# Moving the second input group of each FFN ahead of the first group's turn

## The chip, the cores and the metric

The kernel runs on 1 core of one Trainium2 chip. The metric is device time in microseconds (us) of one execution. Before the change the median of 3 runs is 1911.91 us (1911.91 to 1919.89).

## The reference

The program is a two-layer transformer-like block in fp32 on 256 tokens of width 1024, followed by a second two-layer block. Only the feed-forward networks (FFN) of the first block and what joins them to their neighbours matter here; there are four, two in each layer, with 2816 hidden features:

```python
def rmsnorm(x, g):
    xf = x.astype(jnp.float32)
    y = xf * lax.rsqrt(jnp.mean(xf * xf, axis=-1, keepdims=True) + EPS)
    return (y * g.astype(jnp.float32)).astype(x.dtype)

def swiglu(x, w_in, w_out):
    gate, up = jnp.split(x @ w_in, 2, axis=-1)
    return (jax.nn.silu(gate) * up) @ w_out
...
    for i in range(DEPTH):
        g = norm_g[i]
        h = h + 0.5 * rmsnorm(swiglu(rmsnorm(h, g[0]), ffn1_w_in[i], ffn1_w_out[i]), g[1])
        u = rmsnorm(h, g[2])
        j = i // 2
        if i % 2 == 0:
            mix = even_mixer(u, even_w_in[j], even_w_out[j], lb_all[j], hgrn_onorm_g[j], attn_sinks[j], cos_b, sin_b)
        else:
            mix = odd_mixer(u, odd_w_in[j], odd_w_out[j], ret_onorm_g[j], cos_c, sin_c)
        h = h + rmsnorm(mix, g[3])
        h = h + 0.5 * rmsnorm(swiglu(rmsnorm(h, g[4]), ffn2_w_in[i], ffn2_w_out[i]), g[5])
        gate = jax.nn.sigmoid(h @ ple_w_gate[i])
        h = h + rmsnorm(gate * (p[i] @ ple_w_proj[i]), g[6])
```

The second block (pooling mixer, attention, two squared-ReLU MLPs) follows. Its adaptive scales, a product of a vector with a large matrix (`adw`), are worked out in the background of the first block.

## The kernel before

**Products.** Every fp32 product is made of three matmuls on halves of the operands. `split` loads a 128x1024 piece of weights (raw tile, SP's queue), casts it on ACT to the high half `wh` (line 232) and subtracts on DVE to get the low half `wl` (two instructions, line 235). `mm3` (lines 239 to 241) issues high x high, high x low, low x high. The weight ring holds 7 split pieces, the raw ring 4.

**The normalised input.** A residual update ends in a `junction`: for each of the two rows of 128 tokens (t = 0, 1), `step(t)` squares the result on ACT (`rstd`, line 291, tile jkm), multiplies and adds on DVE (tiles yt and h) and calls `feed`. That transposes h on PE (tile tps) and writes high and low halves of the feature-major input xT (lines 335 and 336), multiplied by the norm's gain but not yet by the row's scale 1/rms. The scale comes from `stats(x, t)`: one square of the whole row with its sum on ACT (line 343, tile jkg), then an addition and a power on POOL (lines 344 and 345, tile rx). In the kernel before, both calls of `stats` stand at the end of step(1), tied behind the last copy of the feed on ACT. The argument `act` adds a one-element activation (`warm`, line 352) behind the feed of t = 0, to load a function table; the junction of the PLE block of layer 0 gives it, that of the even mixer does not.

**An FFN** (`ffn`) has 11 pairs of 128 hidden features. The first pair is worked out token-major: `group512` makes gate and up for 256 features in tile g (a PSUM accumulator), ACT applies silu with the row's scale (line 467), DVE multiplies (line 468, tile sil), and `t_split` transposes the result on PE (line 416) and splits it into hid (lines 244 and 245). The last step is called the turn of the first group in the title; it waits for x.r. Then `rb_of` spreads the scales over a tile rb: two diagonal tiles dg on DVE (line 400), two fp32 products with ones on PE (line 401, tile rbp; four entries in the profile) and a copy on ACT (line 403). The other ten pairs (`inp`) are feature-major: for each of two halves j a bank finm takes 48 matmuls (two weight pieces), DVE multiplies by rb (line 482), ACT applies silu (line 483), DVE multiplies by the up half (line 484), and the result is split into hid. The output of a pair (`out_kn`, tile acc, 24 matmuls) follows one pair behind.

**Buffers.** finm, rbp and all tps come from one pool of two PSUM banks (`pwk`); a bank is free again when its last reader is through. g and acc share another pool of two. sil has 2 buffers.

**Order.** The order of the instructions in each engine's queue is made by a planner from the order of the program (a lower place comes first), the dependences and its own reckoning of durations; a queue, once made, runs in that order. `issue_after` adds an edge within an engine's queue.

**In the background**, `side_ada` streams pieces of `adw` (raw tile rawa, 2 buffers) through DVE (line 974, tile jka) beside each FFN, with a low place in the order, after a silu of the vectors sv on ACT (line 979).

The printed lines are those of the profile.

Of the kernel before, what the change touches and what calls it, by code (L numbers as in the profile page):

```python
# [9 lines left out]
F32 = mybir.dt.float32  # L10
# [3 lines left out]
AF = mybir.ActivationFunctionType  # L14
ALU = mybir.AluOpType
# [154 lines left out]
def tile_model(ctx: ExitStack, tc: tile.TileContext, A, out):  # L170
    nc = tc.nc
    V, S, G, T, Y = nc.vector, nc.scalar, nc.gpsimd, nc.tensor, nc.sync
# [70 lines left out]
    def hilo(hi, lo, src):  # L243
        ins = S.activation(hi, src, AF.Copy)  # L244
        V.tensor_tensor(lo, src, hi.bitcast(F32), op=ALU.subtract)  # L245
        return ins.ins
# [5 lines left out]
    def bank(r=None, name="bk"):  # L252
        r = r or M
        return r.bank.tile([128, 512], F32, name=name + r.tag, tag="bk" + r.tag)
# [25 lines left out]
    def gload(row):  # L280
        return bc(row, 1024, tp, "gb", tag="gb", bufs=1)

    def stat(name):
        return tp.tile([128, 1], F32, name=name, tag=name, bufs=10 if name == "ex" else 6)

    def ssq2(halves, scale):
        sm = small(2, "sm2")
        for n in range(2):
            r = cur[0]
            jk = r.small.tile([128, 512], BF16, name="jk" + r.tag, tag="jk" + r.tag, bufs=1)  # L290
            S.activation(jk, halves[n], AF.Square, scale=scale, accum_out=sm[:, n:n + 1])
        return sm

    def ms_r(sm, e, st=False):
        ms = stat("msx") if st else small(1, "ms")
        V.scalar_tensor_tensor(ms, sm[:, 0:1], sm[:, 1:2], e, op0=ALU.add, op1=ALU.add)
        r = stat("rx") if st else small(1, "rs")
        ins = G.tensor_tensor(r, ms, nhalf[:, :1], op=ALU.pow)
        return ms, r, ins.ins if hasattr(ins, "ins") else ins

    def halves(x):
        return [x[:, 512 * n:512 * n + 512] for n in range(2)]
# [36 lines left out]
    def stats(x, t):  # L339
        if x.stats:  # L340
            sm, ms, r = stat("smx"), stat("msx"), stat("rx")
            jk = tp.tile([128, 1024], BF16, name="jkg", tag="yt", bufs=3)
            S.activation(jk, h[:, t], AF.Square, scale=1.0 / 32, accum_out=sm)
            G.tensor_scalar(ms, sm, EPS, None, op0=ALU.add)
            G.tensor_tensor(r, ms, nhalf[:, :1], op=ALU.pow)
            x.ms[t], x.r[t] = ms, r

    def after(ins):
        return tc.issue_after(ins) if ins is not None else nullcontext()

    def warm(f):
        S.activation(dummy[:, 0:1], dummy[:, 1:2], f)

    def junction(acc, gb, mul, e, x, g, pre=None, act=None):
        def rstd(t):
            sm = ssq2(halves(acc[t]), 1.0 / (32 * mul))
            return ms_r(sm, e[t] if e is not None else epst[:, (0 if mul == 1.0 else 1):(1 if mul == 1.0 else 2)])[1:]

        def scaled(t, n):
            sl = slice(512 * n, 512 * n + 512)  # L360
            y = tp.tile([128, 512], F32, name="yt", tag="yt", bufs=3)
            V.tensor_tensor(y, acc[t][:, sl], gb[:, sl], op=ALU.mult)
            return y

        def add(t, n, y, r):
            sl = slice(512 * n, 512 * n + 512)
            return V.scalar_tensor_tensor(h[:, t, sl], y, r, h[:, t, sl], op0=ALU.mult, op1=ALU.add).ins

        done_ = [None]

        def step(t):
            with after(done_[0]):
                if pre is not None:
                    pre(t)
                r, _ = rstd(t)
                ys = [scaled(t, n) for n in range(2)]
                for n in range(2):
                    with after(done_[0]):
                        done_[0] = add(t, n, ys[n], r)
                    if x.xt is not None:  # L380
                        ins = feed(x, t, n, g)
            if x.xt is not None and t == 0:
                with tc.issue_after(ins):
                    if act is not None:
                        warm(act)
            if t == 1:
                if x.xt is None:
                    for t in range(2):
                        stats(x, t)
                elif x.stats:  # L390
                    with tc.issue_after(ins):
                        for t in range(2):
                            stats(x, t)
        return step

    def rb_of(x):
        ps = bank(name="rbp")
        for t in range(2):
            dg = tp.tile([128, 128], F32, name="dg", tag="dg", bufs=2)
            V.tensor_scalar(dg, ident, x.r[t], None, op0=ALU.mult)  # L400
            T.matmul(ps[:, 128 * t:128 * t + 128], ones, dg, start=True, stop=True)
        rb = tp.tile([128, 256], F32, name="rb", tag="rb", bufs=1)
        S.activation(rb, ps[:, 0:256], AF.Copy)
        return rb
# [6 lines left out]
    def t_split(src, nk, xt, t, k0=0, r=None):  # L411
        for q in range(0, nk, 4):
            n = min(4, nk - q)
            ps = bank(r, "tps")
            for i in range(n):
                T.transpose(ps[:, 128 * i:128 * i + 128], src[:, 128 * (q + i):128 * (q + i) + 128], ident)
            p3 = ps[:, :128 * n].rearrange("p (k c) -> p k c", c=128)
            sl = (slice(None), slice(k0 + q, k0 + q + n), slice(128 * t, 128 * t + 128))
            hilo(xt[0][sl], xt[1][sl], p3)

    def acc_tiles():
        return [pacc.tile([128, 1024], F32, name="acc", tag="acc") for _ in range(2)]
# [35 lines left out]
    def ffn(x, win, wout, np_, pool, hooks, joint):  # L458
        def first():
            hid = xt_tiles(2, pool, "hid", 4)  # L460
            ps = group512(win[0:2], x.xt, True)
            for t in range(2):
                if x.r[t] is None:
                    stats(x, t)
            for t in range(2):
                s = pool.tile([128, 256], F32, name="sil", tag="sil", bufs=2)
                S.activation(s, ps[:, t, 0:256], AF.Silu, scale=x.r[t])
                V.tensor_tensor(s, s, ps[:, t, 256:512], op=ALU.mult)
                t_split(s, 2, hid, t)
            return hid  # L470

        hids = [first()]
        rb = rb_of(x)

        def inp(i):
            hid = xt_tiles(2, pool, "hid", 4)
            for j in range(2):
                ps = bank(name="fin")
                for u in range(2):
                    feat_tile(ps[:, 256 * u:256 * u + 256], split(M, win[2 * i + j], u), x.xt)  # L480
                s = pool.tile([128, 256], F32, name="sil", tag="sil", bufs=2)
                V.tensor_tensor(s, ps[:, 0:256], rb, op=ALU.mult)
                S.activation(s, s, AF.Silu)
                V.tensor_tensor(s, s, ps[:, 256:512], op=ALU.mult)  # L484
                hilo(hid[0][:, j, :], hid[1][:, j, :], s)
            return hid

        acc = None
        for i in range(1, np_):
            hids.append(inp(i))  # L490
            if i in hooks:
                hooks[i](pool)
            if acc is None:
                acc = acc_tiles()
            k = i - LAG
            if 0 <= k < np_ - 2 - XF:
                out_kn(wout[k], acc, hids[k], 0, k == 0, False)
        for k in range(np_ - LAG, np_ - 2 - XF):
            out_kn(wout[k], acc, hids[k], 0, k == 0, False)
        out_multi([(wout[j], hids[j], 0) for j in range(np_ - 2 - XF, np_)], acc, False, True, joint(acc), XF, pool)  # L500
# [112 lines left out]
    def even_block(l, x, nx, ng):  # L613
# [5 lines left out]
        with tc.tile_pool(name="ev", bufs=1, reuse_waits="tile") as ev:  # L619
# [214 lines left out]
            gb = gload(A["norm_g"][l, 3])  # L834
# [3 lines left out]
            for b in range(2):  # L838
# [3 lines left out]
            acc = acc_tiles()  # L842
            x2 = nx()
            out_kn(A["evo"][0], acc, yts[0], 0, True, False)
            out_kn(A["evo"][2], acc, ys, 0, False, False)
            out_multi([(A["evo"][3], ys, 2), (A["evo"][1], yts[1], 0)], acc, False, True,
                      junction(acc, gb, 1.0, None, x2, ng))
        return x2

    def odd_block(l, x, nx, ng):  # L850
# [682 lines left out]
    x = new_x()  # L1533
# [15 lines left out]
    for l in range(2):  # L1549
        x = ffn_block(l, 1, x, new_x, gcol[:, l, 1], cuts[l, 1], None if l else {2: setup, 5: rope2})  # L1550
        x = (odd_block if l else even_block)(l, x, new_x, gcol[:, l, 2])
        x = ffn_block(l, 2, x, plain, None, cuts[l, 2], {5: fin0} if l else None)
# [33 lines left out]
        x = ple_block(l, x, last if l else new_x, None if l else gcol[:, 1, 0], mid if l else None)  # L1586
# [27 lines left out]
```

## Time and profile before

| what | value |
|---|---|
| median of 3 runs | 1911.91 us (1911.91 to 1919.89) |
| the profiled execution | 1917.58 us, span of its instructions 1915.7 us |
| PE (matmul) busy | 1840.0 us, 96% of the span |
| DVE busy | 1336.4 us, 70% |
| ACT busy | 924.9 us, 48% |
| POOL busy | 57.1 us, 3% |
| mean granted TensorE clock | 0.990 |
| read from HBM | 353.03 MB, 185 GB/s over the span |

The page is of one execution; its own time and not the median belongs to its rows. Matmul ends are modelled, so that a busy PE can be a PE that waits within a matmul; stretches of idle time and the granted clock are measured. The four FFNs lie at about 9 to 200, 323 to 517, 552 to 752 and 953 to 1152 us of the span.

### The profile page before, as it was taken

How to read it: one execution, taken by the hardware profiler on the slowest of the kernel's cores; microseconds unless marked ns; L12 is line 12 of the kernel's file. 1: busy time of each engine (PE TensorE's matmuls, PEld its weight loads, DVE VectorE, ACT ScalarE, POOL GpSimd, SP SyncE). 2: the span in 40 equal slices, each digit the busy share in tenths (PEclk: the TensorE clock that was granted, in tenths of full speed). 3: DMA queues.
4: the chain of work that ended last, by engine and by line, in shares of the span. 5: the costliest groups of instructions: out<-in, count | busy, mean ns of one | idle time of the engine just before them, and what ended most of it. 6: DMA issues, size and time to landing. Idle time of an engine off the chain costs nothing.

```text
span 1915.7 us, 29706 instructions
## 1 busy us (share of the span) xinstructions
PE 1840.0 (96%) x11425; PEld 1616.8 (84%) x11425; DVE 1336.4 (70%) x2531; ACT 924.9 (48%) x1452; POOL 57.1 (3%) x96
## 2 busy tenths in 40 slices
PE   8999999999989999999989999899999999999998
PEld 6999777899869998788789897798899987667997
DVE  7997767998679976765587767854444468656555
ACT  6544766544474445444454355632232335544443
POOL 0000000000000000000000000100000002000000
PEclk9999999999999999999999999999999999999999
DMA  8886534887568866655588867332333324216662
GB/s 281 287 280 224 174 112 145 272 285 250 176 205 275 280 215 203 212 168 164 162 275 287 296 207 263 122 121 92 97 91 108 100 67 134 90 56 188 198 191 84
DMA packets 100949, 356.06 MB, mean 186 GB/s; under 512 B 12248, under 2 KB 13128, under 8 KB 100808
## 3 DMA queue, kind: packets, MB, share of 16 engines
q1 hardware_dynamic: 100088, 353.30, 56.8%
q8 instruction: 89, 1.46, 0.3%
q10 hardware_dynamic: 720, 0.88, 0.1%
q14 instruction: 52, 0.43, 0.1%
HBM read 353.03 MB, written 1.10 MB: 185 GB/s over the span
## 4 chain that ended last, share of the span: by engine, by line
PE 77%; DVE 8%; DMA 7%; ACT 3%; issue 2%; POOL 1%; SPq 0%; POOLq 0%; ACTq 0%; DVEq 0%
PE acc L239 8%; PE acc L241 8%; PE acc L240 8%; PE finm L239 6%; PE finm L240 6%; PE finm L241 6%; DMA rawa<-in_adw_dram 4%; PE mfinm L239 3%; PE mfinm L240 3%; PE mfinm L241 3%; DVE wlm L235 3%; PE g L239 2%; PE g L241 2%; PE g L240 2%; PE cfof L239 2%
## 5 line engine op out<-in xcount | busy, mean ns | idle before, releaser
L235 DVE TENSOR_TENSOR wlm<-rawm,whm 128x512 fp32r<-128x512 f32 x1048 | 682.7, 685 | 326.0 <-ACT whm L232 323.2
L232 ACT ACTIVATE whm<-rawm 128x1024 fp32r<-128x1024 f32 x524 | 549.6, 1058 | 522.7 <-PE acc L241 139.7
L239 PE MATMUL finm<-xTh,whm 128*128 128x256 f32 x1280 | 359.9, 281 | 5.4 <-DVE sil L484 5.4
L240 PE MATMUL finm<-xTl,whm 128*128 128x256 f32 x1280 | 359.2, 281 | 0.0
L241 PE MATMUL finm<-xTh,wlm 128*128 128x256 f32 x1280 | 359.1, 281 | 0.0
L239 PEld LDWEIGHTS finm<-xTh,whm 128*128 128x128 f32 x1280 | 240.7, 188 | 8.6 <-DVE sil L484 7.1
L241 PEld LDWEIGHTS finm<-xTh,wlm 128*128 128x128 f32 x1280 | 245.1, 192 | 0.0
L240 PEld LDWEIGHTS finm<-xTl,whm 128*128 128x128 f32 x1280 | 240.4, 188 | 1.3
L239 PE MATMUL acc<-whm,hidh 128*128 128x512 f32 x544 | 214.4, 394 | 2.6 <-ACT hidh L244 2.6
L974 DVE SCALAR_TENSOR_TENSOR jka<-rawa,sv 128x1024 bf16<-128x1024 f32 x160 | 194.9, 1218 | 30.9 <-DMA rawa<-in_adw_dram 29.8
L241 PE MATMUL acc<-whm,hidl 128*128 128x512 f32 x544 | 214.1, 394 | 0.0
L240 PE MATMUL acc<-wlm,hidh 128*128 128x512 f32 x544 | 213.8, 393 | 0.0
L239 PE MATMUL g<-whm,xTh 128*128 128x512 f32 x320 | 130.6, 408 | 10.8 <-ACT xTh L335 4.2
L240 PE MATMUL mfinm<-xTl,whm 128*128 128x256 f32 x480 | 132.6, 276 | 0.0
L241 PE MATMUL mfinm<-xTh,wlm 128*128 128x256 f32 x480 | 132.6, 276 | 0.0
L239 PE MATMUL mfinm<-xTh,whm 128*128 128x256 f32 x480 | 132.6, 277 | 0.0
L241 PE MATMUL g<-whm,xTl 128*128 128x512 f32 x320 | 130.5, 408 | 0.3 <-DVE xTl L250 0.2
L240 PE MATMUL g<-wlm,xTh 128*128 128x512 f32 x320 | 128.7, 402 | 0.0
L239 PEld LDWEIGHTS acc<-whm,hidh 128*128 128x128 f32 x544 | 103.1, 190 | 24.3 <-ACT hidh L244 4.3
L241 PEld LDWEIGHTS acc<-whm,hidl 128*128 128x128 f32 x544 | 102.8, 189 | 21.3 <-DVE hidl L245 0.5
L240 PEld LDWEIGHTS acc<-wlm,hidh 128*128 128x128 f32 x544 | 103.0, 189 | 20.6 <-DVE wlm L235 0.3
L240 PEld LDWEIGHTS mfinm<-xTl,whm 128*128 128x128 f32 x480 | 90.2, 188 | 0.6
(466 smaller groups left out, 3125.9 us busy)
## 6 DMA issues: line engine op xcount, KB each, us to landing
rawm<-in_m_dram SPq DMA_DIRECT2D x128, 512.0 KB, 3.8
rawa<-in_adw_dram SPq DMA_DIRECT2D x96, 512.0 KB, 5.6
rawm<-in_f1i_dram SPq DMA_DIRECT2D x88, 512.0 KB, 4.9
rawm<-in_f2i_dram SPq DMA_DIRECT2D x88, 512.0 KB, 4.9
rawm<-in_odi_dram SPq DMA_DIRECT2D x48, 512.0 KB, 4.2
rawm<-in_f1o_dram SPq DMA_DIRECT2D x40, 512.0 KB, 6.0
rawm<-in_f2o_dram SPq DMA_DIRECT2D x40, 512.0 KB, 5.3
rawm<-in_evi_dram SPq DMA_DIRECT2D x22, 512.0 KB, 4.1
```

What stands on the lines that cost most here:

```text
L232: S.activation(wh, src, AF.Copy)
L235: V.tensor_tensor(wl[:, sl], src[:, sl], wh[:, sl].bitcast(F32), op=ALU.subtract)
L239: T.matmul(o, a[0], b[0], start=first, stop=False)
L240: T.matmul(o, a[0], b[1], start=False, stop=False)
L241: T.matmul(o, a[1], b[0], start=False, stop=last)
L974: V.scalar_tensor_tensor(jk, src, 1.0, sv[v], op0=ALU.mult, op1=ALU.mult, accum_out=adacol[:, l, v, 2 * i + f:2 * i + f + 1])
```

## The change

In `ffn` the turn is cut off from `first()` and called after the input part of the second pair, `inp(1)`; `rb_of` is called within `inp(1)`, behind the matmuls of its first half. The sil tile gets four buffers in place of two. In `junction`, where x is fed, the `stats` of row 0 is called within step(1), behind the squares of that step, and only that of row 1 stays behind the last feed. The junction of the even mixer is given act=Silu. The first FFN makes its scales in `first()`, before and after the change. The rest is as before.

```diff
@@ junction, step(t)
                 r, _ = rstd(t)
+                if t == 1 and x.xt is not None and x.stats:
+                    stats(x, 0)
                 ys = [scaled(t, n) for n in range(2)]
...
                 elif x.stats:
                     with tc.issue_after(ins):
-                        for t in range(2):
-                            stats(x, t)
+                        stats(x, 1)
@@ ffn
+            ss = []
             for t in range(2):
-                s = pool.tile([128, 256], F32, name="sil", tag="sil", bufs=2)
+                s = pool.tile([128, 256], F32, name="sil", tag="sil", bufs=4)
                 S.activation(s, ps[:, t, 0:256], AF.Silu, scale=x.r[t])
                 V.tensor_tensor(s, s, ps[:, t, 256:512], op=ALU.mult)
-                t_split(s, 2, hid, t)
-            return hid
-
-        hids = [first()]
-        rb = rb_of(x)
+                ss.append(s)
+
+            def turn():
+                for t in range(2):
+                    t_split(ss[t], 2, hid, t)
+            return hid, turn
+
+        h0, turn = first()
+        hids = [h0]
+        rbs = []
...
-                s = pool.tile([128, 256], F32, name="sil", tag="sil", bufs=2)
-                V.tensor_tensor(s, ps[:, 0:256], rb, op=ALU.mult)
+                s = pool.tile([128, 256], F32, name="sil", tag="sil", bufs=4)
+                if not rbs:
+                    rbs.append(rb_of(x))
+                V.tensor_tensor(s, ps[:, 0:256], rbs[0], op=ALU.mult)
...
             hids.append(inp(i))
+            if i == 1:
+                turn()
@@ even_block
-                      junction(acc, gb, 1.0, None, x2, ng))
+                      junction(acc, gb, 1.0, None, x2, ng, act=AF.Silu))
```

## Rows read from the trace of the kernel before

**Rows 1.** The page, chain that ended last: share of the span by engine.

```profile
PE 77%; DVE 8%; DMA 7%; ACT 3%; issue 2%; POOL 1%; SPq 0%; POOLq 0%; ACTq 0%; DVEq 0%
```

**Rows 2.** Stretches: us; PE, PEld, DVE, ACT, POOL busy (instructions); clock, DMA share, GB/s.

```profile
24.57:29.62 5.05, 3.27 (x16) 2.24 (x16) 3.82 (x9) 4.07 (x7) 0.00 (x0) 1.00 0.88 311
337.65:346.88 9.23, 5.46 (x17) 4.25 (x17) 7.27 (x16) 7.43 (x11) 1.49 (x3) 0.63 0.87 296
565.92:575.65 9.73, 5.76 (x20) 4.31 (x19) 8.97 (x18) 6.96 (x11) 1.11 (x3) 0.65 0.79 268
967.65:975.69 8.04, 4.23 (x16) 3.17 (x16) 6.44 (x18) 6.31 (x13) 2.81 (x6) 0.79 0.67 219
373.16:378.61 5.45, 5.45 (x27) 4.52 (x25) 5.45 (x12) 2.96 (x4) 0.00 (x0) 1.00 0.81 265
378.61:384.26 5.65, 5.65 (x49) 5.65 (x48) 5.65 (x11) 2.12 (x2) 0.00 (x0) 1.00 0.77 249
```

**Rows 3.** Timeline of turn B: start, us, engine, line, out<-in, [idle before <-releaser].

```profile
338.03 1.28 ACT L467 ACT_TABLE_LOAD   x1
339.33 0.47 ACT L467 ACTIVATE sil<-g,rx 128x256 f32<-128x256 f32 x1
...
340.94 0.69 PE L416 MATMUL tpsm<-identt,sil 128*128 128x128 f32 x2 [3.29 <-DVE sil L468]
341.67 0.38 ACT L244 ACTIVATE hidh<-tpsm 128x256 fp32r<-128x256 f32 x1 [0.92 <-PE tpsm L416]
342.11 0.79 PE L239 MATMUL acc<-whm,hidh 128*128 128x512 f32 x1 [0.47 <-ACT hidh L244]
...
344.40 1.06 PE L401 MATMUL rbpm<-dg,ones 128*128 128x128 f32 x4
345.50 0.39 ACT L403 ACTIVATE rb<-rbpm 128x256 f32<-128x256 f32 x1 [0.47 <-PE rbpm L401]
```

**Rows 4.** Timeline of the turns A, C and D.

```profile
26.79 0.50 PE L239 MATMUL acc<-whm,hidh 128*128 128x512 f32 x1 [0.69 <-ACT hidh L244]
28.18 0.61 PE L401 MATMUL rbpm<-dg,ones 128*128 128x128 f32 x4
30.01 0.37 ACT L403 ACTIVATE rb<-rbpm 128x256 f32<-128x256 f32 x1
...
569.41 0.69 PE L416 MATMUL tpsm<-identt,sil 128*128 128x128 f32 x2 [3.49 <-DVE sil L468]
...
972.42 0.79 PE L239 MATMUL acc<-whm,hidh 128*128 128x512 f32 x1 [0.26 <-ACT hidh L244]
973.43 1.06 PE L401 MATMUL rbpm<-dg,ones 128*128 128x128 f32 x4
974.90 0.38 ACT L403 ACTIVATE rb<-rbpm 128x256 f32<-128x256 f32 x1
```

**Rows 5.** Timeline of two joints: into the even mixer, and into FFN B.

```profile
206.74 0.37 ACT L335 ACTIVATE xTh<-tpsm,gct 128x128 fp32r<-128x128 f32 x1 [3.05 <-PE tpsm L327]
210.04 1.05 ACT L343 ACTIVATE jkg<-h 128x1024 bf16<-128x1024 f32 x1
...
325.04 0.50 PE L239 MATMUL g<-whm,xTh 128*128 128x512 f32 x1 [0.65 <-ACT xTh L335]
327.41 1.06 ACT L232 ACTIVATE whx<-rawx 128x1024 fp32r<-128x1024 f32 x1 [1.08 <-DMA rawx<-in_f2o_dram]
```

**Rows 6.** FFN B, timeline; FFN D: timeline, a stretch, waits from 977 to 1105.

```profile
443.96 0.42 DVE L484 TENSOR_TENSOR sil<-sil,finm 128x256 f32<-128x256 f32 x1
451.25 0.28 PE L239 MATMUL finm<-xTh,whm 128*128 128x256 f32 x1
...
1059.33 0.39 PE L239 MATMUL finm<-xTh,whm 128*128 128x256 f32 x1 [1.11 <-DVE sil L484]
...
1040.00:1105.00 65.00, 59.58 (x426) 55.02 (x425) 49.92 (x92) 25.66 (x36) 0.00 (x0) 1.00 0.85 292
...
DVE jka L974 <- DMA rawa<-in_adw_dram: 21.6, 14, 2.7
```

## The prediction

> **What bounds the kernel now.** I read the chain of work that ended last first: PE holds 77% of it [rows 1]. So the kernel ends when PE ends, a stretch in which PE stands still is paid in full, and everything else is free as long as it stays behind PE. Next I looked through PE's timeline for idle time at the four places that the diff touches, the end of the first input group of each FFN. I call the stretch from the last matmul of that group (tile g) to the first full-speed matmul of the second group (tile finm) the turn. The stretches view gives the four turns 5.05, 9.23, 9.73 and 8.04 us [rows 2], in the order of the program (FFN 1 and 2 of layer 0, FFN 1 and 2 of layer 1; A, B, C, D below). The granted clock column of the same rows says 1.00, 0.63, 0.65 and 0.79. Time at the lower level (0.5, that is 1.2 GHz) is twice the missing share: 2 x 0.37 x 9.23 = 6.8 us in B, 6.8 in C, 3.4 in D, none in A.
>
> What would PE have needed for the work that it did in there? At 2.4 GHz 24 matmuls into acc take 5.45 us, 0.227 each, and 48 into finm take 5.65, 0.118 each [rows 2]. Four rb matmuls take 1.06 us at 1.2 GHz [rows 3] and 0.61 at 2.4 [rows 4]; the step that doubles is (1.06 - 0.61)/4, 0.11 us, and a transpose has the same shape. Between the two ends of B's turn PE ran 4 transposes, 4 rb matmuls and 8 acc matmuls: 8 x 0.11 + 8 x 0.227 = 2.7 us of work in 9.23. So B loses 6.5. By the same count A (8 small, 7 acc) loses 5.05 - 2.5 = 2.6, C (8 small, 7 acc, 3 finm) 9.73 - 2.8 = 6.9, and D (9 small, 6 acc) 8.04 - 2.4 = 5.6. Together 21.6 us.
>
> The timeline of B shows why [rows 3]: PE waits 3.29 us for the gated tile sil, with the 1.28 us load of the silu table in the middle of that wait; then 0.47 for the first hidh; then it runs at half clock. In C there is no table load, and PE still waits 3.49 [rows 4]: squares, rx, silu and product run one after the other behind weight casts.
>
> **The change, part by part.**
>
> *The second group ahead of the turn.* The 48 matmuls of its first half (5.65 us) are put into the place of the wait. Their input xT has been complete since the first group, and a bank is free, since the transposes of the first group no longer ask for both. The chain to the gated tile (3.3 to 3.5 us) fits under 5.65, so the wait for sil goes, and with it, I take it, the idle stretch after which the clock fell. Gain: the 21.6 us above, before what is put in their place.
>
> *What is late next.* The rb matmuls now stand in PE's queue between the halves of the second group, and the bank pool has two tiles: finm holds one, rbp the other. So the second half must wait until ACT has copied rb, because the first half's own bank is only released after two products and a silu that need rb too. Queued behind this wait on PE are the second half, the turn and acc; nothing else can run there. Before, acc matmuls covered it. Price: from the end of rbp to the start of the copy 1.22 us in A, 0.04 in B and 0.41 in D [rows 3, 4], mean 0.56; the copy 0.38; 0.06 from ACT's end to PE's start (hidh ends 0.06 before acc starts). 1.0 us a turn, between 0.5 and 1.7. Then the turn itself: transposes, hidh, first acc matmul, with nothing left to cover it. That wait was 0.69, 0.47 and 0.26 us [rows 3, 4]; I keep the mean, 0.47, with 0.26 and 1.5 (0.47 and one weight cast of 1.06 ahead on ACT [rows 5]) as ends. So each turn costs 1.47, four cost 5.9, and the ends are 3.0 and 12.8. Two more sil buffers cost no instruction. The rb matmuls also need both rx. Before, they ran 3.6 (A), 6.8 (B) and 5.8 us (D) after the group's end [rows 2 to 4], behind transposes and acc in the queue, which bounds the time of rx from above; against 5.65 for the first half, and with one of the two squares moved up, I count no wait (at worst 1.1 in B, 0.1 in D).
>
> *The squares of tile row 0.* In five joints one square of 1.05 us on ACT [rows 5], and its two small POOL steps, move from behind the last feed to before the second row's. Where the joint leads into a mixer, ACT sits idle for 3.05 us just there [rows 5]: no cost. In B's joint ACT's idle is 1.08 before a cast [rows 5], and PE is already 0.65 late for a feed there. So between 0 and 1.05 per joint; I put 0.3 on C's and nothing on D's, where the tail has slack of the same kind.
>
> *The table load of B.* 1.28 us [rows 3] and a 128x1 activation with it move from the turn, where they would now be hidden anyway, into the joint, where the feeds of PE stand behind them on ACT. Bounds 0 and 1.28 plus the square's 1.05, 2.3 together; less the idle of 1.08 and what the weight casts behind can give way, I take 0.8. The gain of the move is nil: after the reordering PE has 5.65 us of cover for a chain of 3.3. The Trainium skill ("ScalarE: Activation LUTs", What ACT_TABLE_LOAD costs) prices a switch at about 2.66 us, a load and a drain as long again. The row disagrees: silu started 0.02 us after the 1.28 us load [rows 3]. By the page's figure the joint's bound would be 3.7 instead of 2.3.
>
> *Who gives it back.* A turn that is shorter only pays if the rest of that FFN runs at PE's pace. PE needs a bank that DVE has emptied (L484). In B, where the two come closest behind an output, that product ended at 444.38 and the group that takes its bank started at 451.25 [rows 6]: 6.9 us between, more than the 4 to 5 that PE will gain. In D it is the other way: from 1040 to 1105 PE is busy only 59.58 of 65 us, DMA moves 292 GB/s, and PE waits for that very product (1.11 us at 1059.33) [rows 6], because DVE stands in order behind jka, which waits for the transfers of rawa (14 waits, 21.6 us [rows 6]). A PE that comes 4.1 us earlier meets this wall earlier. Unless the rawa stream starts earlier too, D's gain is lost; I keep 1.5 of 4.1, between 0 and 4.1.
>
> **Sum.** A 2.6 - 1.47 = 1.1; B 6.5 - 1.47 - 0.8 = 4.2; C 6.9 - 1.47 - 0.3 = 5.1; D 1.5. Together 11.9, taken as 12.0 us of the profiled execution's 1917.58 (span 1915.7 and 1.9 around it), which would be 1905.6. The median of the runs is 5.7 lower; the gain is the same, 1911.9 - 12.0 = **1899.9**.
>
> **The rivals.**
>
> *D keeps its gain.* If the rawa stream moves up with PE: 2.6 more, 1897.3. For it: the silu of sv, which starts the stream, stands on ACT behind work of the turn. Against: 292 GB/s.
>
> *A new wait takes the old one's place.* If rb stands behind two casts (2 x 1.06) and the turn's hidh behind one, a turn costs 2.6 + 1.5 = 4.1. A then loses 1.5, B and C keep 1.6 and 2.5, D nothing: 2.6 gained, 1909.3. A's 1.22 us speaks for it, B's 0.04 against.
>
> *The clock falls at the short waits too.* Each turn has two new stops at banks. If each turn fell to 1.2 GHz for 3.4 us, as D did, it would lose 1.7 us of work: 4 x 1.7 = 6.8, a gain of 5.2, 1906.7. Against it: the stretch 1040 to 1105, with several bank waits, was granted 1.00 throughout [rows 6]. The Trainium skill states this rule ("TensorE: Matmul & The Clock Gate", A second HAM failure mode: psum-queue depth-cycling): short idles between groups that cycle through PSUM banks make the clock swing between its two levels. By that rule 1906.7; the stretch just named doesn't show it.
>
> *It doesn't do what it says.* The planner orders each queue by its own reckoning; if the transposes get the bank first, the order on PE stays. Then 1912 or so.
>
> *Slower.* The place is ACT's queue in the joints. If the square (and in B the load) goes ahead of feeds that PE waits for, five joints lose 1.05 each, B's 1.28 more, 6.5 together; and if those longer stops bring 6.8 us at half clock each, 3.4 lost, another 17. Against the 12.0 gained that is 1923.4. It decides from 12 us on, 2.4 per joint. The 0.65 of B's joint speaks for it; ACT's idle of 3.05 in two of the five against.
>
> **How the numbers follow.** Forecast 0.47; D keeps its gain 0.15; new wait 0.16; clock at short waits 0.06; order unchanged 0.08; slower 0.08. A measurement of this kernel tells about 0.5% from no change, 9.6 us: below 1902.3 is faster. The forecast's own bounds: turns 3.0 instead of 5.9 and no joint cost, with D whole, would give 18.6 (1893.3); turns at 1.47 with B's joint at 2.3 and D at nil give 8.9 (1903.0). A quarter of its chance lies above 1902.3. Faster: 0.35 of the forecast, 0.14 of the second, some 0.04 of the others, 0.53. Slower 0.07; the rest, 0.40, within 0.5%. The range runs from 1891 (18.6 gained, and 2 for a queue order that falls better elsewhere) to 1910, which takes in the new wait; order unchanged and slower, 0.16, lie outside.
>
> **What would show each step.** After the end of g, PE should go on with finm without a stop; the granted clock of turns B, C and D should be 1.00; between the two halves there should be one PE wait released by ACT rb, near 1 us; at the transposes one by ACT hidh near 0.5. The stall of D at 1058 to 1103 should grow by what its turn gave. ACT should show the table load in B's joint, next to a square. Wrong: PE idle of over 2 us at rb, half clock in the turns or the joints, transposes still ahead of finm.

## The result and the profile after

The changed kernel took 1929.55 us, median of 6 runs (1926.49 to 1934.58), against 1913.61 of the kernel before on the same chip (1911.91 to 1919.89): ratio 1.0079, 95% interval 1.0062 to 1.0096. It is slower by 0.8%; 1899.9 us was predicted, in a range up to 1910. The profiled execution took 1930.06 us with a span of 1928.3, 12.6 longer than that of the kernel before, and the mean granted clock is 0.987 in place of 0.990.

The chain that ended last answers to [rows 1]. PE is still the bound, with a point less:

```profile
PE 76%; DMA 8%; DVE 8%; ACT 4%; issue 3%; POOL 1%; SPq 0%; POOLq 0%; ACTq 0%; DVEq 0%
```

To compare a turn before and after, a stretch is needed that holds the same work on both sides: from the end of tile g to the first matmul of the third input group, that is 96 matmuls into finm, 24 into acc, four rb matmuls and four transposes. The stretches view of A to D, first of the kernel before, then of the changed one (start:end, length, busy us of PE, PEld, DVE, ACT, POOL, clock, DMA share, GB/s):

```profile
24.57:44.39 19.82, 18.05 (x130) 16.33 (x129) 15.49 (x39) 13.79 (x20) 0.00 (x0) 1.00 0.85 298
337.65:361.86 24.21, 20.45 (x129) 18.56 (x129) 20.65 (x40) 14.21 (x20) 1.49 (x3) 0.86 0.76 249
565.92:590.07 24.15, 20.18 (x130) 18.05 (x129) 19.82 (x39) 13.73 (x20) 1.11 (x3) 0.86 0.76 253
967.65:991.08 23.43, 19.62 (x130) 17.86 (x130) 20.48 (x43) 15.39 (x25) 2.81 (x6) 0.93 0.78 258
```

```profile
24.84:50.82 25.98, 20.72 (x129) 18.93 (x128) 20.33 (x51) 15.85 (x25) 0.00 (x0) 0.87 0.79 262
345.08:370.11 25.03, 20.28 (x129) 17.87 (x129) 20.90 (x41) 11.63 (x18) 0.00 (x0) 0.86 0.81 266
576.03:600.15 24.12, 19.42 (x129) 17.61 (x128) 19.43 (x38) 11.54 (x18) 0.00 (x0) 0.93 0.80 265
980.22:1003.56 23.34, 19.73 (x130) 18.18 (x130) 18.59 (x35) 12.68 (x20) 0.28 (x2) 0.93 0.77 250
```

Nothing was gained in C and D, B lost 0.8 us and A 6.2. Yet the wait at the end of g, 3.29 us in [rows 3] and 3.49 in [rows 4], is gone: in all four turns PE goes on with finm at once. It stands still later, at two places (in B the second has two waits). The timeline of A shows both (start, us, engine, line, out<-in, idle before and what ended it):

```profile
30.13 0.60 PE L402 MATMUL rbpm<-dg,ones 128*128 128x128 f32 x4
30.44 1.06 ACT L232 ACTIVATE whm<-rawm 128x1024 fp32r<-128x1024 f32 x1 [1.53 <-DMA rawm<-in_f1i_dram]
31.77 1.06 ACT L232 ACTIVATE whm<-rawm 128x1024 fp32r<-128x1024 f32 x1 [0.28 <-DMA rawm<-in_f1i_dram]
32.73 0.36 ACT L404 ACTIVATE rb<-rbpm 128x256 f32<-128x256 f32 x1
33.15 0.58 PE L239 MATMUL finm<-xTh,whm 128*128 128x256 f32 x1 [2.42 <-ACT rb L404]
...
38.76 1.28 ACT L616 ACT_TABLE_LOAD   x1
40.38 0.39 PE L417 MATMUL tpsm<-identt,sil 128*128 128x128 f32 x2
40.50 1.06 ACT L232 ACTIVATE whm<-rawm 128x1024 fp32r<-128x1024 f32 x1
41.58 1.28 ACT L492 ACT_TABLE_LOAD   x1
43.19 0.36 ACT L244 ACTIVATE hidh<-tpsm 128x256 fp32r<-128x256 f32 x1
43.61 0.80 PE L239 MATMUL acc<-whm,hidh 128*128 128x512 f32 x1 [2.85 <-ACT hidh L244]
```

First stop: rb stands on ACT behind two weight casts, each of which waits for its transfer, and the second half of the group waits for the bank that rb's copy frees. Second stop: hidh stands behind a cast, the silu table load and the second half's silu; the silu table has to be loaded because the set-up work had just loaded exp's. What stands next in PE's queue is acc, which needs hidh, so PE waits. In C there is no table load, and the second stop is longer:

```profile
587.75 1.22 DVE L985 SCALAR_TENSOR_TENSOR jka<-rawa,sv 128x1024 bf16<-128x1024 f32 x1 [2.02 <-DMA rawa<-in_adw_dram]
588.55 0.38 PE L417 MATMUL tpsm<-identt,sil 128*128 128x128 f32 x2
589.24 1.22 DVE L985 SCALAR_TENSOR_TENSOR jka<-rawa,sv 128x1024 bf16<-128x1024 f32 x1
590.38 1.29 DVE L235 TENSOR_TENSOR wlm<-rawm,whm 128x512 fp32r<-128x512 f32 x2
591.59 0.42 DVE L491 TENSOR_TENSOR sil<-finm,rb 128x256 f32<-128x256 f32 x1
592.04 0.42 ACT L492 ACTIVATE sil<-sil 128x256 f32<-128x256 f32 x1 [2.30 <-DVE sil L491]
592.36 0.36 ACT L244 ACTIVATE hidh<-tpsm 128x256 fp32r<-128x256 f32 x1
592.78 0.79 PE L239 MATMUL acc<-whm,hidh 128*128 128x512 f32 x1 [3.84 <-ACT hidh L244]
```

Read it from the bottom: acc waits for hidh, hidh stands on ACT behind a silu, the silu waits for a product on DVE, and the product stands behind two jka, the first of which waited 2.02 us for its transfer, and two subtractions of weights (wlm). The half clock is there again too: 0.50 or 0.51 in these stretches, two in A and one each in B, C and D:

```profile
33.20:36.40 3.20, 3.20 (x15) 3.20 (x16) 2.68 (x9) 0.83 (x2) 0.00 (x0) 0.50 0.76 244
43.60:46.70 3.10, 3.09 (x8) 2.48 (x9) 2.19 (x8) 0.80 (x2) 0.00 (x0) 0.51 0.89 342
360.70:367.50 6.80, 5.09 (x13) 4.08 (x14) 6.73 (x14) 1.22 (x3) 0.00 (x0) 0.50 0.70 204
592.80:596.20 3.40, 3.40 (x9) 2.71 (x10) 2.72 (x6) 0.80 (x2) 0.00 (x0) 0.50 0.86 280
988.70:992.20 3.50, 3.50 (x17) 3.50 (x18) 2.04 (x5) 0.88 (x3) 0.00 (x0) 0.51 0.93 324
```

PE was busy for 18.3 of these 20.0 us, so that the half clock lost some 9.1, half of it (an estimate from these rows).

**Where the 12.6 us came from.** The table below cuts PE's timeline at landmarks that both kernels have: A, B and C reach from the end of g to the start of the next stage, "joint" from g's first matmul to its last, "odd" is the odd mixer, D its joint and FFN together, "rest" everything else, "span" that of the profile. Each number is the difference to the profiled execution of the kernel before, in us, and each row is one execution, on several chips. A scatters by some 4 us between executions: the changed kernel and the runs 1, 7 and 8 have the same instructions in the same order in A (run 1 up to the joint at its end), and lie between +6.1 and +10.4. The other columns scatter too. Runs 6, 7 and 8 have the queues of the changed kernel, instruction for instruction, in the odd mixer and in D; odd lies between -2.3 and +2.1 there, D between -3.6 and +3.9. Run 6 has them in B as well (-0.5 against +0.7), runs 6 and 8 in C (0.0 to +1.5). A single difference within this scatter shows nothing.

| run | A | joint B | B | joint C | C | odd | D | rest | span |
|---|---|---|---|---|---|---|---|---|---|
| changed kernel | +6.1 | +1.2 | +0.7 | +2.0 | 0.0 | +2.1 | -0.3 | +0.8 | +12.6 |
| 1 turn only | +8.9 | 0.0 | -3.2 | 0.0 | -2.3 | -0.7 | +0.8 | +0.9 | +4.4 |
| 2 joint only | +2.1 | +1.1 | -1.8 | +2.2 | -0.5 | +1.3 | -4.7 | +1.3 | +0.8 |
| 3 other banks | -0.9 | +1.4 | -5.5 | +1.9 | -2.3 | +0.5 | +5.0 | -1.1 | -0.9 |
| 4 between | -2.3 | 0.0 | -7.4 | 0.0 | -6.9 | -0.3 | -4.6 | +1.2 | -20.3 |
| 5 split first | +4.6 | +1.6 | -0.8 | +2.0 | +1.2 | +2.8 | +0.3 | -1.1 | +10.6 |
| 6 set-up later | +5.5 | +1.0 | -0.5 | +2.4 | +0.4 | -2.3 | +3.9 | -0.2 | +10.2 |
| 7 stream held | +8.9 | +1.3 | -4.0 | +3.5 | -3.4 | +0.9 | -1.5 | -1.1 | +4.7 |
| 8 no early silu | +10.4 | +1.2 | -4.3 | +2.0 | +1.5 | +1.7 | -3.6 | -1.6 | +7.3 |
| 9 between, joint | -2.7 | +1.6 | -7.4 | +2.1 | -7.1 | -0.4 | -1.9 | +1.0 | -14.8 |
| 10 two stages | -2.4 | 0.0 | -7.4 | 0.0 | -6.5 | -2.4 | -4.1 | -0.2 | -23.0 |
| 11 less in D | +3.5 | 0.0 | -7.2 | 0.0 | -6.9 | -2.0 | -8.3 | -1.3 | -22.3 |
| 12 dealt again | -2.1 | 0.0 | -7.2 | +0.4 | -6.5 | -2.9 | -6.1 | +0.8 | -23.5 |

### The profile page after: what moved, and what is told of

The parts are those of the page before. It is cut to its first block, busy times and chain, and to the rows that moved or that the text cites. A ratio compares the mean times of both kernels' runs of the same rounds, so it can differ in the third digit from the quotient of the medians.

```text
span 1928.3 us, 29657 instructions
## 1 busy us (share of the span) xinstructions
PE 1848.0 (96%) x11425; PEld 1621.4 (84%) x11425; DVE 1336.2 (69%) x2531; ACT 924.3 (48%) x1453; POOL 59.0 (3%) x96
## 4 chain that ended last, share of the span: by engine, by line
PE 76%; DMA 8%; DVE 8%; ACT 4%; issue 3%; POOL 1%; SPq 0%; POOLq 0%; ACTq 0%; DVEq 0%
PE acc L241 8%; PE acc L239 8%; PE acc L240 8%; PE finm L239 6%; PE finm L240 6%; PE finm L241 6%; DMA rawa<-in_adw_dram 5%; PE mfinm L240 3%; PE mfinm L239 3%; PE mfinm L241 3%; DVE wlm L235 3%; PE g L239 2%; PE g L241 2%; PE g L240 2%; PE cfof L239 2%
## 5 line engine op out<-in xcount | busy, mean ns | idle before, releaser
L240 PEld LDWEIGHTS acc<-wlm,hidh 128*128 128x128 f32 x544 | 103.6, 190 | 21.6 <-DVE wlm L235 0.6
L239 PEld LDWEIGHTS mfinm<-xTh,whm 128*128 128x128 f32 x480 | 90.5, 189 | 0.7
```

The costliest lines, as they stand in the source:

```text
L239: T.matmul(o, a[0], b[0], start=first, stop=False)
L240: T.matmul(o, a[0], b[1], start=False, stop=False)
```

## The experiments

Theory 1: the wait for the gated result was moved, not removed; what comes after it on PE now waits for rb and for hidh, which ACT and DVE bring late, and PE has nothing to do meanwhile. Rivals: the part in the joints makes the loss (theory 2 below); ACT and DVE can't work faster anyway (theory 3).

**Run 1, the turn only.** The joints are put back as they were:

```diff
-                if t == 1 and x.xt is not None and x.stats:
-                    stats(x, 0)
...
-                        stats(x, 1)
+                        for t in range(2):
+                            stats(x, t)
...
-                      junction(acc, gb, 1.0, None, x2, ng, act=AF.Silu))
+                      junction(acc, gb, 1.0, None, x2, ng))
```

> The change without its part in the joints: the squares of tile row 0 stand behind the last feed again and the silu table load of B is back behind g. Theory 1 (the wait for the gated result was moved and not removed: PE now stops between the halves for rb, and at the first product into acc for hidh, with nothing left in its queue that it could do): turn A, which no joint feeds, loses the 5.5 to 6 us that it lost in the changed kernel, turns B to D gain 0 to 3 each, and the two joints give back 1.1 and 2.0; time 2 to 9 us above the kernel before. Rival 2 (the squares and the table load in the joints make the loss): within 3 us of the kernel before, or faster.

Ratio to the kernel before 1.0019 (1.0003 to 1.0035). By the medians that is 2.2 us slower, which theory 1 (2 to 9) and the rival (within 3) both allowed; the stretches decide. The turn alone gains nothing: B and C gain 3.2 and 2.3, A loses more than that. But the rest of the loss, from 0.2% to 0.8%, needs the part in the joints as well, and not in the joints alone: with it, B and C lose 3.9 and 2.3 us *behind* g.

**Run 2, the joint only.** The kernel before with the lines that run 1 takes out.

> The kernel before with the part in the joints alone (squares of row 0 early, silu table load in the joint of B). Theory 1: the joints of B and C get 1.1 and 2.0 us longer, the table load of 1.28 us is gone from the 3.29 us wait of turn B, so B gets shorter by about 1; net 0 to 4 us slower than the kernel before. Rival 2: 10 us slower or more.

Ratio 1.0025 (1.0010 to 1.0039), 4.4 us by the medians, a little over what was expected. The joints lose 1.1 and 2.2 us, as in the changed kernel, and B is 1.8 shorter. So theory 2 is out as the whole, and in as a part: 0.2% and 0.25% alone, 0.8% together.

**Run 3, other banks.** The changed kernel, rbp and tps in another pool:

```diff
-        ps = bank(name="rbp")
+        ps = bank(AD, "rbp")
...
-                    t_split(ss[t], 2, hid, t)
+                    t_split(ss[t], 2, hid, t, r=AD)
```

> The changed kernel with rbp and the turn's two tps in the two PSUM banks of the mixers, which stand empty in an FFN; finm keeps both banks of its own pool. Theory 1a (a good half of the new waits is the bank: the second half of the input group can't start before rb is copied): the waits for rb of 2.42, 0.96, 0.86 and 2.22 us go; those for hidh (2.85, 3.79 in two pieces, 3.84, 1.39) get shorter where finm of the third half can stand ahead of acc; time 6 to 12 us below the changed kernel, that is 2 below to 8 above the kernel before. Rival 2 (joints): at most 3 us below the changed kernel. If the stops at banks only move to another tile of the same engines ACT and DVE: 0 to 3 below the changed kernel.

Ratio 1.0005 (0.9988 to 1.0021), more below the changed kernel than the 6 to 12 us expected: by the spans 13.5. The waits for rb are gone in all four turns; A is 7.0 and B 6.2 shorter than in the changed kernel. The waits for hidh stay, 1.54, 1.16, 2.97 and 1.89 us, although seven to ten matmuls of the third group now stand ahead of acc. D is 5.0 us longer, with a stop of 10.73 us at a small transpose (adt) that the planner now puts there.

**Run 4, between.** Without the part in the joints, and the turn between the halves of the second group:

```diff
+                tp2 = bank(AD, "tps")
                 for t in range(2):
-                    t_split(ss[t], 2, hid, t)
+                    for k in range(2):
+                        T.transpose(tp2[:, 256 * k + 128 * t:256 * k + 128 * t + 128],
+                                    ss[t][:, 128 * k:128 * k + 128], ident)
+                hilo(hid[0].rearrange("p k c -> p (k c)"), hid[1].rearrange("p k c -> p (k c)"), tp2)
...
                 if not rbs:
+                    turn()
                     rbs.append(rb_of(x))
...
-            if i == 1:
-                turn()
```

rbp stands in the other pool, as in run 3.

> Without the part in the joints, and with the turn between the halves of the second input group: half 1 of finm, four transposes into one bank of the mixers' pool, four rb matmuls into the other, half 2 of finm, acc. Here 5.65 us of matmuls cover the gated result, and 5.65 us more cover rb and hid. Theory 1: all four turns run at 2.4 GHz without a wait of over 0.5 us; gain 2.6 in A, 6.5 in B, 6.9 in C, 1.5 in D, at most 17.5 together; time 10 to 18 us below the kernel before. If ACT and DVE can't work faster anyway (theory 3, the stop comes back later at a bank in the same FFN): 0 to 5 below. Rival 2: like the first run of this call.

Ratio 0.9930 (0.9903 to 0.9957), 1898.19 us against 1914.63. The stretches of its four turns, 17.5 us each from the end of g:

```profile
24.98:42.48 17.50, 17.50 (x128) 16.54 (x128) 13.71 (x32) 10.65 (x16) 0.00 (x0) 1.00 0.77 240
335.55:353.05 17.50, 17.50 (x132) 16.55 (x132) 15.08 (x29) 13.56 (x20) 1.44 (x3) 1.00 0.80 272
556.30:573.80 17.50, 17.50 (x130) 16.55 (x130) 15.41 (x31) 12.32 (x19) 0.98 (x3) 1.00 0.80 268
949.39:966.89 17.50, 17.50 (x133) 16.55 (x132) 15.89 (x31) 13.46 (x22) 2.80 (x6) 1.00 0.86 300
```

PE is busy for 17.50 of 17.50 us, at clock 1.00. What took 19.8 to 24.2 us before takes 17.1 to 17.5. The gains of A, B and C, 2.3, 7.4 and 6.9, are those that the prediction counted before its deductions (2.6, 6.5, 6.9), and the other kernels with this turn (runs 9 to 12) repeat each within 0.6, but for A in run 11. In D the turn is 6.3 us shorter (23.43 to 17.10), D as a whole 4.6. The work and the engines are those of the changed kernel. What differs is the place of the turn, with a half of the group behind it that covers rb and hidh; the banks, which run 3 has alone; the joints, which run 9 puts back; and that a turn makes hidh and hidl in one instruction each in place of two, which no run has alone. That confirms theory 1 and rules out theory 3 for A to C.

**Run 5, split first.** The changed kernel, hidh and hidl ahead of the second half's gating:

```diff
+                a, v = turn() if i == 1 and j == 1 else (None, None)
+                with after(a), after(v):
-                V.tensor_tensor(s, ps[:, 0:256], rbs[0], op=ALU.mult)
+                    V.tensor_tensor(s, ps[:, 0:256], rbs[0], op=ALU.mult)
...
```

> The changed kernel, and in each turn hidh and hidl are put ahead of the gating of the second half (product with rb, silu, product) in the queues of ACT and DVE. PE's order is the same. Theory 1 (hidh and hidl come late because they stand behind that gating): the waits for hidh in B (1.13 and 2.66) and C (3.84) fall to 1.0 us or less each turn, D's 1.39 to about 0.5, A's 2.85 by the silu table load (1.28) that stands ahead of hidh, while the exp load stays ahead of it; with less half clock, 5 to 9 us below the changed kernel. If it is rather the wait of jka for its transfer, which stands ahead of both on DVE: B and C shrink by less than 1 us each, time within 3 us of the changed kernel.

Ratio 1.0043 (1.0024 to 1.0061). By the ratios that is some 7 us below the changed kernel, inside the 5 to 9 expected; by the profiled executions it is 2.0, with B 1.5 shorter and C 1.2 longer, within the scatter. For the waits this part of theory 1 held only by half: the one for hidh in C went down from 3.84 to 1.13, and 3.26 us came up one step on, at the second pair of transposes. PE waits there for a bank, and the bank for hidl, which is behind two jka and three subtractions of weights on DVE:

```profile
586.27 1.23 DVE L992 SCALAR_TENSOR_TENSOR jka<-rawa,sv 128x1024 bf16<-128x1024 f32 x1 [2.80 <-DMA rawa<-in_adw_dram]
587.76 1.22 DVE L992 SCALAR_TENSOR_TENSOR jka<-rawa,sv 128x1024 bf16<-128x1024 f32 x1
588.90 1.90 DVE L235 TENSOR_TENSOR wlm<-rawm,whm 128x512 fp32r<-128x512 f32 x3
590.71 0.43 DVE L481 TENSOR_TENSOR hidl<-tpsm,hidh 128x256 fp32r<-128x256 f32 x1
591.19 0.69 PE L477 MATMUL tpsm<-identt,sil 128*128 128x128 f32 x2 [3.26 <-DVE hidl L481]
```

**Run 6, set-up later.** The changed kernel with one number changed: `{2: setup, 5: rope2}` becomes `{4: setup, 5: rope2}`.

> The changed kernel, with the set-up work of FFN A (rope angles on DVE, two exp activations on ACT that load the exp table and let the next silu load its own again) called after the fourth input group in place of the second. Theory 1: the wait for hidh in A falls from 2.85 us to 1 or less, and its half clock with it; 2 to 4 us below the changed kernel, nothing else moves by over 1 us. If the table loads don't matter (hidh waits for weight casts alone): A's wait stays above 2 us.

Ratio 1.0052 (1.0037 to 1.0068). A's wait for hidh fell from 2.85 to 1.43 us, but A is only 0.6 shorter: in this execution its wait for rb was 3.56 in place of 2.42. So the table loads make half of the second stop here; the first, rb behind casts that wait for transfers, is the one that scatters (2.42 to 5.33 over the executions with that order), and run 3 showed that freeing the bank removes it. That nothing else would move by over 1 us didn't hold: with the queues of the changed kernel B has a wait for rb of 2.46 in place of 0.96, and D is 4.2 longer.

**Run 7, stream held.** The changed kernel; in B and C the background stream starts behind the turn's last hidh and hidl:

```diff
+            def held(ins):
+                if chunks and (l, f) in HELD:
+                    with after(ins[0]), after(ins[1]):
+                        side_ada(pool, chunks)
...
             if i == 1:
-                turn()
+                held(turn())
```

> The changed kernel, with the background stream (silu of sv on ACT, jka on DVE) of FFNs B and C held until the turn's hidh and hidl are through; A and D as changed. If the wait of jka for its transfers is what delays hidh and hidl in B and C (theory 1b): the waits there, 1.13 and 2.66 in B, 3.84 in C, fall to 1.5 us or less in each turn, 4 to 7 us below the changed kernel, unless the later stream brings stops further on. If the gating and the casts alone do it: under 1 us less each. The rb waits (0.96 and 0.86) stay in both.

Ratio 1.0037 (1.0025 to 1.0049). B and C are 4.7 and 3.4 us shorter than in the changed kernel. C's wait for hidh is 1.43, and its chain has a cast and the silu in it, and no jka:

```profile
588.13 0.38 PE L478 MATMUL tpsm<-identt,sil 128*128 128x128 f32 x2
588.26 1.06 ACT L233 ACTIVATE whm<-rawm 128x1024 fp32r<-128x1024 f32 x1 [1.71 <-PE finm L241]
589.22 0.40 ACT L500 ACTIVATE sil<-sil 128x256 f32<-128x256 f32 x1
589.53 0.36 ACT L481 ACTIVATE hidh<-tpsm 128x256 fp32r<-128x256 f32 x1
589.94 0.50 PE L240 MATMUL acc<-whm,hidh 128*128 128x512 f32 x1 [1.43 <-ACT hidh L481]
```

So jka ahead of the gating, waiting for rawa, made most of the second stop in C. In B 1.13 and 2.66 became 1.44; run 6, with the queues of the changed kernel there, had 1.13 and 0.53, so for B it is less sure, though B is 3.5 us shorter than in run 6 too. The rb waits stayed (1.25 and 1.33).

**Run 8, no early silu.** The changed kernel without `act=AF.Silu` in the even mixer's joint.

> The changed kernel without act=Silu in the even mixer's joint; the squares of row 0 stay early. Only B should move. If the early table load is what lets the silu of sv, and with it jka, start early in B: the first jka comes 2 to 4 us later after the end of g, the wait of 2.66 us at the second transposes goes, B gets 2 to 4 us shorter, and its joint by 0 to 1; C and its joint as in the changed kernel. If the squares do it: B within 1 us of the changed kernel.

Ratio 1.0062 (1.0044 to 1.0080), by itself not to be told from the changed kernel. B is 5.0 us shorter (3.8 against run 6) and its wait of 2.66 is gone; the joint of B is as long as with the load (+1.2). So there the early table load costs nothing that shows, and the squares do. What the load does is to let the silu of sv run early: 1.48 us after the end of g in the changed kernel, 4.40 here and 5.59 in run 1; the first jka follows at 3.86, 5.79 and 7.53. In C the early squares do the same: sv 0.87 us before the end of g instead of 3.44 after it in run 1.

**Run 9, between, with the joint.** Run 4 with the lines of run 2.

> The run with the turn between the halves, with the part in the joints as the change has it. If the price of the part in the joints is paid in the joints alone: the stretch from the first to the last matmul of g gets longer by 1.1 in B and 2.0 in C, the start of the odd mixer by 1 to 2, the turns keep 17.5 us; 4 to 6 us above that run. If the part in the joints hurts the turns too, by starting the background stream earlier (theory of the interaction: the turns of B and C lost 4.0 and 2.3 us more with it than without it): in this kernel, whose turns are covered, that loss doesn't show, so again 4 to 6; a loss of 8 or more would speak for another path.

Ratio 0.9953 (0.9936 to 0.9969), 0.23% above run 4, with intervals that overlap. The turns keep their gain; the joints cost 1.6 and 2.1, and D is 2.7 longer, within its scatter. Where the turn is covered, an early stream does it no harm.

**Runs 10 to 12, FFN D.** In run 4 PE waits 7.43 us in D for the second of two small transposes, whose input tile has one buffer. Run 10 gives it two:

```diff
-            stage = pool.tile([128, 4, 8], F32, name="stage", tag="stage", bufs=1)
+            stage = pool.tile([128, 4, 8], F32, name="stage", tag="stage", bufs=2)
```

> The run with the turn between the halves, and tile stage (32 columns, two copies in place of one), so that the second small transpose adt in FFN D no longer waits for the first to be read. There it made PE wait 7.43 us at 1029 of the span. Theory 1 has that stop as an accident of the queue and no bound of D: it goes, time 5 to 9 us below the run with the turn between the halves, 18 to 25 below the kernel before. If FFN D is bound by DVE and the transfers of rawa, as I had put it (D keeps only 1.5): the stop comes back as waits of finm for sil, and the time is within 3 us of that run.

Ratio 0.9898 (0.9877 to 0.9919), some 6 us below run 4, with intervals that overlap; by the spans it is 2.6. So the time doesn't decide. The stop went, and D stayed at -4.1 (run 4: -4.6): it came back as waits of finm for sil. Runs 11 and 12 deal the pieces of adw out again, in place of 9, 11, 10 and 15:

```diff
-    cuts = {(0, 1): lat[:9], (0, 2): lat[9:20], (1, 1): lat[20:30], (1, 2): lat[30:45], (1, 0): lat[45:]}
+    cuts = {(0, 1): lat[:10], (0, 2): lat[10:22], (1, 1): lat[22:34], (1, 2): lat[34:45], (1, 0): lat[45:]}
```

> The run with the turn between the halves and two stage tiles, and the pieces of adw dealt out 10, 12, 12 and 11 to the FFNs A to D in place of 9, 11, 10 and 15. If D is bound by the stream (jka waits for rawa, finm waits for sil there: 1.77, 2.46, 0.88 and 1.73 us between 1020 and 1102): these stops go, D gets 4 to 8 us shorter; A to C, whose turns had no stop, have room for one to two pieces each; time 3 to 8 us below that run. If the stops in D come from the weights' own transfers: D unchanged within 2 us, A to C no shorter, time the same or longer.

Ratio 0.9911 (0.9895 to 0.9928): 3 to 8 us less than in run 10 were expected, and none came. PE's waits in D, 180 us from the end of g (engine, line, waited for: us, times, longest), in run 10 with 15 pieces and in run 11 with 11:

```profile
PE finm L239 <- DVE sil L497: 7.5, 6, 2.5
```

```profile
PE finm L239 <- DVE sil L497: 2.3, 1, 2.3
```

D went from -4.1 to -8.3, a step within its scatter, and A, with one piece more, from -2.4 to +3.5, with a stop of 3.50 us at which finm waits for sil. Run 12 gives A its nine back:

```diff
+    cuts = {(0, 1): lat[:9], (0, 2): lat[9:21], (1, 1): lat[21:33], (1, 2): lat[33:45], (1, 0): lat[45:]}
```

> The run with the turn between the halves and two stage tiles, and the pieces of adw dealt out 9, 12, 12 and 12. With 10, 12, 12 and 11, D had become 5.3 us shorter than there and A 5.9 longer (a stop of 3.50 at 170 of the span), B and C unchanged. If each FFN has a wall of its own, set by its pieces: A is back at 2 to 3 us below the kernel before, B and C stay 7 below, D gets 3 to 5 shorter than with 15 pieces; 3 to 5 us below that run, 21 to 26 below the kernel before in the span. If the stop in A came of something else than its tenth piece: A stays 3 above the kernel before, and the time is that of that run.

Ratio 0.9889 (0.9866 to 0.9911), 1895.74 us against 1918.67. A is back, B and C as before, D at -6.1, with 12 pieces and this wait:

```profile
PE finm L239 <- DVE sil L497: 5.6, 4, 1.7
```

It has the lowest ratio of the study; run 10's interval holds it too, so of the two nothing is decided. In A, four executions of this turn with nine pieces lie between -2.7 and -2.1, so the one with ten, at +3.5, stands out: nine fit and ten don't. In D fewer pieces go with shorter waits, one execution each. That every FFN has a wall of its own, set by its pieces, fits this, and is not shown.

## Why the prediction was wrong, by its own steps

**What bounds the kernel, and what there was to gain: right.** Of the 21.6 us before deductions, 16.0 were put on A to C; run 4 gained 16.6 there.

**"What is late next": this step failed, by its sizes.** It priced rb at 1.0 us a turn and hidh at 0.47, 5.9 in all. Measured in the changed kernel: rb 2.42, 0.96, 0.86 and 2.22, together 6.5; hidh and the second transposes 2.85, 1.13 + 2.66, 3.84 and 1.39, together 11.9; and the half clock in the stretches shown, which the sum had put at nothing, lost 9.1. That makes 27.5, which is 5.9 more than the 21.6 gained; the four stretches A to D are together 6.9 longer than before. Turn by turn, what the waits and the clock cost less what was counted as gain is +5.8, +0.8, -0.5 and -0.2, and the stretches changed by +6.2, +0.8, 0.0 and -0.1. The range had 0.26 to 1.5 for hidh: the ends were taken from waits of the kernel before, where ACT could be idle until the transposes were through (0.92 us in B [rows 3]). Moved behind the second half, it is wanted at the moment when that half's gating, the next casts and the stream arrive. The price of a wait belongs to its place in the queues and not to the instruction.

**Covers.** I wrote that nothing was left to cover the turn, and priced it as if something were. In A I overlooked the set-up work altogether: its exp load had been behind the turn in ACT's queue and came to stand ahead of it.

**The joints: bounds right for B, too low for C.** B's joint cost 1.2 (priced 0.8 with the load, of which the load was nil, run 8). C's cost 2.0, where I had put 0.3, at most 1.05. I had the square wait for the second row; it went in between the first and the second of row 0's eight copies into xT, and everything that feeds g moved back:

```profile
559.49 0.37 ACT L335 ACTIVATE xTh<-tpsm,gct 128x128 fp32r<-128x128 f32 x1
559.74 1.06 ACT L343 ACTIVATE jkg<-h 128x1024 bf16<-128x1024 f32 x1
560.78 0.63 ACT L335 ACTIVATE xTh<-tpsm,gct 128x128 fp32r<-128x128 f32 x2
561.21 0.50 PE L239 MATMUL g<-whm,xTh 128*128 128x512 f32 x1 [0.32 <-ACT xTh L335]
```

Nor did I ask what the earlier squares and the earlier table would start: the silu of sv, and with it the stream, straight into the turn (runs 7 and 8). The odd mixer's +2.1 I didn't foresee; but with the same queues there run 6 has -2.3, so that no effect is shown.

**D: not tested by the change.** I let D keep 1.5 because of DVE and the rawa stream. In the changed kernel D kept 0.3, but its turn had gained nothing to give back (23.43 to 23.34 us). In runs 4 and 10 the turn gained 6.3 and D 4.6 and 4.1, with waits of 7.4 and 7.5 us further on (finm for sil had 5.4 before). So something was given back, and less than I had deducted; with D's scatter the size stays open.

**The rivals.** "A new wait takes the old one's place" was the mechanism. It was priced at 4.1 us a turn without half clock; the waits alone took 18.4/4 = 4.6, with half clock 6.9. "It doesn't do what it says" is out: PE goes on with finm behind g. The rival for slower had the joints' ACT queue, which gave 3.2 of the 12.6. The rival of the clock had it fall at short waits and lose 6.8 us in the four turns; they lost 9.1. But in the changed kernel's turns the half clock came with the waits of 2.2 us and more; behind the waits of 0.96 in B and 0.86 in C for a bank the stretches view gives clock 1.00:

```profile
350.99:357.50 6.51, 5.55 (x48) 5.55 (x49) 4.27 (x9) 2.80 (x5) 0.00 (x0) 1.00 0.92 332
582.13:588.55 6.42, 5.56 (x49) 5.57 (x49) 4.40 (x8) 2.59 (x5) 0.00 (x0) 1.00 0.88 279
```

The Trainium skill ("TensorE: Matmul & The Clock Gate", A second HAM failure mode: psum-queue depth-cycling) describes a kernel in which short idles between groups that cycle through PSUM banks made the clock swing between its two levels. These two stretches don't show it.

## What to carry to other kernels

Work put ahead of a wait covers it only if the work that follows is also covered: look for the first instruction behind the moved block that needs a result of another engine, and ask what that engine has queued at that moment. Here the remedy was to put the late consumer in the middle of the block and not behind it (run 4), and to give its small tiles a bank of their own (run 3). A step made earlier on a side engine starts whatever was queued behind it, and background work with slow transfers then stands ahead of what is urgent.

## What was not expected of the hardware

A wait of 2.2 to 2.9 us cost between half and nearly as much again by the clock: behind the 2.42 in A, 3.20 us were granted 0.50, as the stretches above show, which lost 1.6; with the 2.22 in D it was 1.75, with the 2.66 in B 2.5 (5.09 us busy at half clock). It is no rule of length: in D of the kernel before, a wait of 2.08 us at 1082.21 left the clock at 1.00, in the stretch of [rows 6].

In the joint of B a 1.28 us table load on ACT cost PE nothing that could be seen, while one square of 1.05 us in the same queue cost 1.2 (1.2 longer with both, 1.2 with the square alone in run 8, 0.0 with neither in run 1).
